# The down weights' block sums move from POOL's queue at the head into the gates' stage, and the fourth activation sum takes one transfer a block instead of two

## The chip, the cores and the metric

One core of one Trainium2 chip runs the whole kernel. The metric is the device time of one execution in microseconds (us), the median of the runs. The engines are TensorE (PE; its weight loads are listed as PEld), VectorE (DVE), ScalarE (ACT), GpSimd (POOL) and SyncE (SP). SP and POOL issue the DMA transfers; POOL issues all those that add to their destination.

## What is computed

One layer of a streaming encoder on 1024 prompt tokens and 64 sample tokens (1088 columns), model width 1024. Cut to what matters:

```python
mk, mv = split(rms_norm(mem, g_mem) @ w_mem_kv)                 # 256 memory tokens
h = rms_norm(x, g_mix_pre)
q, k, v, ca, cb, qm, ga, gb, gc = split(h @ w_in)               # nine widths of 1024
y_sb = stick_breaking(q, k, v) @ w_sb_o
u = ca * sigmoid(cb)                                            # conformer branch
cc = silu(layer_norm(causal_dwconv31(u) + conv_dw_b)); y_conv = cc @ w_conv_o
y_mem = memory_attention(qm, mk, mv) @ w_mem_o
merged = sigmoid(ga) * y_sb + sigmoid(gb) * y_conv + sigmoid(gc) * y_mem
x = x + rms_norm(merged @ w_out, g_mix_post)
up = rms_norm(x, g_ffn_pre) @ w_ffn_up                          # 2 x 2816 channels
fg, fv = split(causal_dwconv3(up))
y = x + rms_norm((gelu(fg) * fv) @ w_ffn_down, g_ffn_post)
```

The last product, (1088 x 2816) times (2816 x 1024), is done in the kernel as a two-by-two block product with seven block multiplications in place of eight. It needs sums of the four blocks of w_ffn_down (A and B are the upper and lower rows of columns 0 to 511, C and E those of columns 512 to 1023) and sums of the blocks of the activations.

## The kernel before, in words

All matrix products run in three passes of rounded halves: a weight block is loaded as `wraw` (SP, line 133), ScalarE casts the high half `whi` (`split`, line 103) and VectorE subtracts to get the low half `wlo` (line 104). `wraw` has three buffers, `whi` and `wlo` two each. `mms` (lines 160 to 162) issues the three matmuls of a step.

The stages, in the order of the program:

- **The head.** The keys and values of the memory tokens (`mem_kv`, matmuls at lines 374 to 376) take 16 blocks of w_mem_kv. Beside the first nine of them one tile of x each is loaded (`x_tile`, line 270), squared on ScalarE (line 276), given its reciprocal root on POOL in two small operations (`rstd_of`, lines 201 and 202, output `rstd_x`; `rstd_mem` for the memory tokens), scaled on VectorE (line 281), and turned on TensorE in groups of four tiles (`turn`, line 291, output `xT`), from which ScalarE and VectorE make the halves `hh` and `hl` of h (lines 107 and 108).
- **The gates' stage.** For each of eight channel blocks i the units cb, ca, qm, ga, gb, and then the eight gc: 48 dense products of h with columns of w_in. After ca of block i, `start_conv` lets POOL write the two edges of the convolution's input `u` (a memset at line 585 and a copy at line 586), and the 31 taps follow bit by bit: the first on ScalarE (line 424), 30 on VectorE (line 427, two at each chunk's end). `u` and its accumulator `acc` have two buffers each. The gc units carry the layer norm's pieces.
- **The attention stage.** `weave.mix` runs the projections of q, k and v and weaves scores, turns and values of the stick-breaking attention in between.
- The branches' output projections, the merge, w_out and the norms.
- **The channel stage.** For 22 blocks f of 128 channels, seven products each (lines 1490 to 1492), the convolution of width 3 (`conv`: POOL copies its edges at lines 1527 to 1529, VectorE taps at line 1532), gelu times value (line 1581), and `put_down`, which writes the block and its sums to DRAM tensors x11, x21, x22, t1 to t4 and small ones for the sample columns (`put` by SP, line 1546; `add`, an accumulating transfer by POOL, line 1549). Blocks 0 to 10 belong to the upper half and put; blocks 11 to 21 add.
- **The down stage**: seven block products (lines 1735 to 1737) that load the sums of weights (`d_w`, shown as d_ws by the profile) and of activations (`d_x`, its t1 to t4 shown as d_xt).

The sums of the weights' blocks are 32 transfers on POOL's queue: for each of s3 = A + C, s1 = C + E, s2 = A + s1 and s4 = B + s2 four plain copies of 352 rows by 512 columns from DRAM to DRAM (line 1123) and then four accumulating ones of the same size onto them (line 1125). An accumulating one must wait for the copy of its rows, and those of s2 and s4 also for the sum they take in. In the program text they are taken from a list one at a time inside `weave.mix`, in the attention stage:

```python
if i % 15 == 7 and down_sums:
    down_sums.pop(0)()
```

The order of instructions on an engine is not that of the text, though. A scheduler sets it by its own costs and by what each instruction depends on, but for places in the text under `tc.manual_schedule`, which keeps the named engine in the text's order. The transfers of the weights' sums depend on inputs alone, and in before the scheduler has put all 32 at the head of POOL's queue, among the rstd operations.

Of the kernel before, what the change touches and what calls it, by code (L numbers as in the profile page):

```python
# [12 lines left out]
ALU = mybir.AluOpType  # L13
# [41 lines left out]
def encoder_step(ctx: ExitStack, tc: tile.TileContext, I, O):  # L55
    nc = tc.nc
    ACT, DVE, POOL, PE, SP = nc.scalar, nc.vector, nc.gpsimd, nc.tensor, nc.sync
# [39 lines left out]
    HK = FF // 2  # L97
    d_w = {j: dp.tile([HK, 512], F32, name=f"d_w{j}") for j in ("s1", "s2", "s3", "s4")}
# [161 lines left out]
    with ExitStack() as st:  # L260
# [152 lines left out]
        def drain(n):  # L413
            owed[0] += n
            while owed[0] >= 1 and bg:
                bg.pop(0)()
                owed[0] -= 1
            owed[0] = min(owed[0], 1.0)

        def conv_ops(i, u):  # L420
            acc = ep.tile([P, 1118], F32, tag="acc", name=f"acc{i}", bufs=2)

            def first():
                ACT.activation(acc, u[:, 0:1118], AF.Identity, bias=cb_c[:, i : i + 1], scale=cw[:, i : i + 1])

            def tap(t):
                DVE.scalar_tensor_tensor(  # L427
                    out=acc, in0=u[:, t : t + 1118], scalar=cw[:, t * 8 + i : t * 8 + i + 1], in1=acc,
                    op0=ALU.mult, op1=ALU.add,
                )  # L430

            def last():
                SP.dma_start(out=d_cc[i * P : (i + 1) * P, 0:TP], in_=acc[:, 0:TP])
                SP.dma_start(out=d_cc[i * P : (i + 1) * P, TP:T], in_=acc[:, 1054:1118])

            return [first] + [lambda t=t: tap(t) for t in range(1, 31)] + [last]

        def conv_state(i, u):
            tp = bank("tr", f"cs{i}")
            PE.transpose(tp[:30, 0:P], u[:, 1024:1054], ident)  # L440
            PE.transpose(tp[:30, P : 2 * P], u[:, 1118:1148], ident)
            cs = ep.tile([30, 2 * P], F32, tag="cs", name=f"cso{i}", bufs=2)
            ACT.copy(out=cs, in_=tp[:30, : 2 * P])
            SP.dma_start(out=O["conv_state_prompt"][0, 0][:, i * P : (i + 1) * P], in_=cs[:, 0:P])
            SP.dma_start(out=O["conv_state_sample"][0, 0][:, i * P : (i + 1) * P], in_=cs[:, P : 2 * P])
# [92 lines left out]
        def step_mem(n=1):  # L538
            for _ in range(n):
                while mem_gens:  # L540
                    try:
                        next(mem_gens[0])
                        break
                    except StopIteration:
                        mem_gens.pop(0)
# [14 lines left out]
        def conv_b(i):  # L560
            sg = ep.tile([P, T], F32, tag="sg", name=f"sg{i}", bufs=1)
            u = ep.tile([P, 1148], F32, tag="u", name=f"u{i}", bufs=2)
            us[i] = (sg, u)

            def evac(ps, t0, n):
                ACT.activation(sg[:, t0 : t0 + n], ps, AF.Sigmoid)

            yield from dense(hT, CH, evac, f"cb{i}")

        def conv_a(i):  # L570
            sg, u = us[i]

            def evac(ps, t0, n):
                for o, m, c in segs(t0, n, 60):
                    c0 = c + 30 if c < TP else c
                    DVE.tensor_tensor(
                        out=u[:, c0 : c0 + m], in0=ps[:, o : o + m], in1=sg[:, t0 + o : t0 + o + m], op=ALU.mult
                    )

            yield from dense(hT, CH, evac, f"ca{i}")  # L580

        def start_conv(i):
            drain(len(bg))
            _, u = us.pop(i)
            POOL.memset(u[:, 0:30], 0.0)
            POOL.tensor_copy(out=u[:, 1054:1084], in_=cst[:, i * 30 : (i + 1) * 30])
            bg.extend(conv_ops(i, u))
            conv_state(i, u)
# [10 lines left out]
        def pace(g, ops):  # L599
            for _ in g:  # L600
                drain(ops)
                step_mem()
# [28 lines left out]
        def ep_tile(kind, shape, name, t):  # L631
# [4 lines left out]
            }[kind][t]  # L636
            return ep.tile(shape, F32, tag=tag, name=name, bufs=bufs)

        live = []
        ticks = 0  # L640
        order = ctx.enter_context(ExitStack())
        for nm, i in units:
            if nm == "cb":
                pace(conv_b(i), 2.2)
            elif nm == "ca":
                pace(conv_a(i), 2.2)
                start_conv(i)
            elif nm == "qm":
                pace(mem_q(i), 2.2)
                if i % 2:  # L650
                    mem_gens.append(mem_attention(i // 2, [qmh[i - 1], qmh[i]], [qml[i - 1], qml[i]]))
            elif nm == "gc":
                if i == 2:
                    order.enter_context(tc.manual_schedule(engines={mybir.EngineType.PE}))
                for end in gate(2, i, dense_steps):
                    if end:
                        step_mem()
                    if bg:
                        if end:
                            drain(3)  # L660
                        continue
                    ticks += 1
                    if ticks % 3 == 0:
                        if len(live) < 4 and len(norms) > 2:
                            live.append((0, layer_norm(norms.pop(0), ep_tile)))
                        if live and live[0][0] <= ticks:
                            g = live.pop(0)[1]
                            if next(g, 0) is None:
                                live.append((ticks + 12, g))
            else:  # L670
                pace(gate(("ga", "gb").index(nm), i), 1.8)
# [6 lines left out]
    with ExitStack() as st:  # L678
# [296 lines left out]
        class Weave:  # L975
# [115 lines left out]
            def mix(self, steps):  # L1091
                for i, _ in enumerate(steps):
                    if i % (3 * NK) == 0:
                        self.work((1024, 1024))
                    if i % 15 == 7 and down_sums:
                        down_sums.pop(0)()
                    self.now += self.STEP
                    while self.left() and self.take():
                        pass
# [12 lines left out]
                self.until(lambda: not self.left())  # L1112

        weave = Weave()


        w_dn = I["w_ffn_down"][0]
        A, B = (w_dn[HK * i : HK * i + HK, 0:512] for i in range(2))
        C, E = (w_dn[HK * i : HK * i + HK, 512:1024] for i in range(2))
        down_sums = []  # L1120
        for j, first, then in (("s3", A, C), ("s1", C, E), ("s2", A, d_w["s1"]), ("s4", B, d_w["s2"])):
            rows = [slice(HK // 4 * i, HK // 4 * i + HK // 4) for i in range(4)]
            down_sums += [lambda j=j, r=r, a=first: POOL.dma_start(out=d_w[j][r, :], in_=a[r, :]) for r in rows]
            down_sums += [
                lambda j=j, r=r, a=then: POOL.dma_start(out=d_w[j][r, :], in_=a[r, :], accum_op=ALU.add, max_dma_last_dim=2048)
                for r in rows
            ]

        def attend(p, S):
            units = []  # L1130
# [83 lines left out]
    op = right.enter_context(tc.tile_pool(name="op", bufs=1, side="right", reuse_waits="tile"))  # L1214
# [203 lines left out]
    for oi, t in enumerate(y_tiles):  # L1418
# [23 lines left out]
        if t not in (0, 2, 5):  # L1442
            then = THEN.get(group[0][0])
# [95 lines left out]
    LEFT, RIGHT, NEW = slice(0, 512), slice(512, 1024), slice(TP + 2, NO)  # L1539

    def put_down(f, g, free):

        r = slice(f % (NF // 2) * P, f % (NF // 2) * P + P)

        def put(j, src):
            SP.dma_start(out=(d_x.get(j) or d_s[j])[r, :], in_=src)

        def add(j, src):
            POOL.dma_start(out=(d_x.get(j) or d_s[j])[r, :], in_=src, accum_op=ALU.add)

        if f < NF // 2:
            put("x11", g[:, LEFT])
            put("x1", g[:, NEW])
            DVE.tensor_tensor(out=free[:, LEFT], in0=g[:, LEFT], in1=g[:, RIGHT], op=ALU.add)
            put("t1", free[:, LEFT])
            ACT.activation(free[:, RIGHT], free[:, LEFT], AF.Copy, scale=-1.0)
            put("t2", free[:, RIGHT])
            put("t4", free[:, RIGHT])
            ACT.activation(g[:, RIGHT.start : NO], g[:, RIGHT.start : NO], AF.Copy, scale=-1.0)
            put("t3", g[:, RIGHT])  # L1560
            put("xd", g[:, NEW])
        else:
            put("x21", g[:, LEFT])
            put("x22", g[:, RIGHT])
            put("x2", g[:, NEW])
            add("t4", g[:, LEFT])
            add("t2", g[:, RIGHT])
            add("t3", g[:, RIGHT])
            add("xd", g[:, NEW])
            add("t4", g[:, RIGHT])  # L1570

    def after(f, j):

# [260 lines left out]
```

## Time and profile before

| what | value |
|---|---|
| median of 3 runs | 2570.61 us (2566.13 to 2572.54) |
| the profiled execution | 2567.92 us |
| its span, first to last instruction | 2566.2 us |
| TensorE busy | 2378.3 us, 93% of the span |
| VectorE busy | 1762.4 us, 69% |
| ScalarE busy | 1101.5 us, 43% |
| POOL busy | 181.7 us, 7% |
| mean DMA rate | 124 GB/s |

The numbers come from one execution, taken by the hardware profiler. Busy time is the time in which an engine executes; register, branch, semaphore and DMA-issuing instructions are not counted in the shares, though the rows of the DMA issues are shown in the order of time. Rows of the page's second part cut the span in 40 slices of 64.2 us and give the busy share in tenths. In rows of groups, "out<-in" names the tiles, without buffer numbers; "A <- B" in the waits means that A's engine sat idle until B ended, "issue" that the profile shows no releaser. Matmuls are pipelined, so their printed durations overlap; the distance between starts is what one costs.

### The profile page before, as it was taken

What the parts mean: (1) busy time and instruction counts of PE and PEld (TensorE: products, weight loads), DVE (VectorE), ACT (ScalarE), POOL (GpSimd) and SP (SyncE); (2) the same over time, 40 slices, a digit from 0 to 9 for tenths busy, and PEclk for the clock granted to TensorE, in tenths of its full rate; (3) what the DMA queues carried; (4) which work ended last, traced back from release to release, by engine and by line L of the source; (5) the groups of instructions that cost most, each with busy time, mean ns of one, the idle gap of its engine ahead of it and who ended that gap; (6) DMA issues with size and microseconds to landing.
All of it is one profiled execution on the core that took longest, in us unless ns stands there. A gap on an engine that the chain in (4) does not pass through costs nothing.

```text
span 2566.2 us, 38158 instructions
## 1 busy us (share of the span) xinstructions
PE 2378.3 (93%) x15035; PEld 2258.1 (88%) x15035; DVE 1762.4 (69%) x2177; ACT 1101.5 (43%) x2035; POOL 181.7 (7%) x350
## 2 busy tenths in 40 slices
PE   2229999999999999999999999999899999998998
PEld 1118999999998999999998999997799999997887
DVE  1115878778786578888888934543898888876555
ACT  2124242424234566666767621213644443334432
POOL 1220000000000000000000000001111112220002
PEclk7569999999999999999999999999999999999999
DMA  7774222222225553333336446522233336659654
GB/s 210 180 171 126 68 72 90 64 90 68 85 65 151 159 134 95 81 88 82 87 95 161 134 139 217 185 92 74 83 107 118 115 112 127 127 97 283 221 179 148
DMA packets 319716, 319.40 MB, mean 124 GB/s; under 512 B 73855, under 2 KB 249107, under 8 KB 319537
## 3 DMA queue, kind: packets, MB, share of 16 engines
q1 hardware_dynamic: 302657, 282.00, 36.0%
q0 software_dynamic: 16880, 34.97, 7.5%
q8 instruction: 118, 1.93, 0.3%
q14 instruction: 61, 0.50, 0.1%
HBM read 206.20 MB, written 112.14 MB: 124 GB/s over the span
## 4 chain that ended last, share of the span: by engine, by line
PE 45%; issue 3%; DVE 2%; ACT 1%; POOL 1%; DMA 1%; DVEq 0%; POOLq 0%; ACTq 0%
PE ff L1490 5%; PE ff L1491 5%; PE ff L1492 5%; PE dn L1735 3%; PE dn L1737 3%; PE dn L1736 3%; PE cv L162 1%; PE sb L162 1%; PE sb L161 1%; PE cv L161 1%; PE cv L160 1%; PE sb L160 1%; PE mo L160 1%; PE mo L161 1%; PE mo L162 1%
## 5 line engine op out<-in xcount | busy, mean ns | idle before, releaser
L427 DVE SCALAR_TENSOR_TENSOR acc<-u,cw,acc 128x1118 f32<-128x1118 f32 x240 | 331.6, 1382 | 5.6
L103 ACT CAST whi<-wraw 128x1024 fp32r<-128x1024 f32 x112 | 118.0, 1054 | 335.4 <-PE cv L161 74.3
L820 DVE TENSOR_TENSOR_SCAN r<-r 128x128 f32<-128x128 f32 (+7 forms) x128 | 173.3, 1355 | 58.6 <-ACT r L816 58.0
L160 PE MATMUL g<-hh,whi 128*128 128x362 f32 (+1 forms) x576 | 193.0, 335 | 0.0
L162 PE MATMUL g<-hh,wlo 128*128 128x362 f32 (+1 forms) x576 | 190.6, 331 | 0.0
L161 PE MATMUL g<-hl,whi 128*128 128x362 f32 (+1 forms) x576 | 190.5, 331 | 0.0
L104 DVE TENSOR_TENSOR wlo<-wraw,whi 128x1024 fp32r<-128x1024 f32 x112 | 136.5, 1219 | 42.3 <-ACT whi L103 39.8
L1502 DVE TENSOR_TENSOR mf<-mf,ff 128x548 f32<-128x548 f32 (+1 forms) x161 | 110.3, 697 | 48.4 <-PE ff L1492 48.3
L376 PE MATMUL mkv<-wlo,mh 128*128 128x512 f32 x64 | 28.9, 459 | 114.2 <-DVE wlo L104 114.2
L1532 DVE SCALAR_TENSOR_TENSOR mf<-mf,fw 128x1090 f32<-128x1090 f32 x88 | 118.9, 1351 | 17.5 <-ACT mf L1530 16.6
L1735 PE MATMUL dn<-wh,xh 128*128 128x512 f32 x308 | 121.0, 393 | 6.7 <-ACT xh L103 6.6
L1737 PE MATMUL dn<-wh,xl 128*128 128x512 f32 x308 | 120.7, 392 | 0.3 <-DVE xl L104 0.3
L1736 PE MATMUL dn<-wl,xh 128*128 128x512 f32 x308 | 120.7, 392 | 0.2 <-DVE wl L104 0.2
L376 PEld LDWEIGHTS mkv<-wlo,mh 128*128 128x128 f32 x64 | 14.4, 225 | 118.9 <-DVE wlo L104 115.5
L815 ACT ACTIVATE be<-z 128x128 f32<-128x128 f32 (+2 forms) x192 | 95.7, 499 | 41.0 <-PE z L844 24.6
L160 PEld LDWEIGHTS g<-hh,whi 128*128 128x128 f32 x576 | 109.8, 191 | 0.2
L161 PEld LDWEIGHTS g<-hl,whi 128*128 128x128 f32 x576 | 109.4, 190 | 0.1
L162 PEld LDWEIGHTS g<-hh,wlo 128*128 128x128 f32 x576 | 109.1, 189 | 0.0
L104 DVE TENSOR_TENSOR atl<-aT,ath 128x512 fp32r<-128x512 f32 (+1 forms) x160 | 99.5, 629 | 10.0 <-ACT ath L103 9.1
L103 ACT CAST ath<-aT 128x512 fp32r<-128x512 f32 (+1 forms) x160 | 87.1, 550 | 42.6 <-PE aT L871 26.8
L281 DVE TENSOR_SCALAR x<-x,rstd_x 128x1024 f32<-128x1024 f32 (+1 forms) x9 | 6.8, 752 | 143.6 <-POOL rstd_x L202 142.8
L104 DVE TENSOR_TENSOR xl<-dr,xh 128x1024 fp32r<-128x1024 f32 (+1 forms) x42 | 47.6, 1134 | 76.4 <-ACT xh L103 76.1
(549 smaller groups left out, 8070.8 us busy)
## 6 DMA issues: line engine op xcount, KB each, us to landing
wraw<-in_w_in SPq DMA_DIRECT2D x72, 512.0 KB, 4.0
d_ws<-in_w_ffn_down POOLq DMA_DIRECT2D x24, 704.0 KB, 6.9
d_gate<-gt SPq DMA_DIRECT2D x24, 544.0 KB, 3.0
vw<-in_w_ffn_up SPq DMA_DIRECT2D x22, 512.0 KB, 3.9
gw<-in_w_ffn_up SPq DMA_DIRECT2D x22, 512.0 KB, 3.8
d_xt<-mf SPq DMA_DIRECT2D x44, 256.0 KB, 2.4
d_xt<-mf POOLq DMA_DIRECT2D x44, 256.0 KB, 6.3
dr<-d_ws SPq DMA_DIRECT2D x20, 512.0 KB, 4.5
```

The source lines that it names most:

```text
L103: ACT.copy(out=hi, in_=src)
L104: DVE.tensor_tensor(out=lo, in0=src, in1=hi.bitcast(F32), op=ALU.subtract)
L160: PE.matmul(ps, wh[:, k, :], rh[k][c], start=first, stop=False)
L161: PE.matmul(ps, wh[:, k, :], rl[k][c], start=False, stop=False)
L162: PE.matmul(ps, wl[:, k, :], rh[k][c], start=False, stop=last)
L427: DVE.scalar_tensor_tensor(out=acc, in0=u[:, t : t + 1118], scalar=cw[:, t * 8 + i : t * 8 + i + 1], in1=acc, op0=ALU.mult, op1=ALU.add,)
L820: DVE.tensor_tensor_scan(out=rv, data0=rv, data1=rv, initial=1.0, op0=ALU.mult, op1=ALU.min)
L1490: PE.matmul(ps, w[:, k, :], xh[:, k, :], start=k == 0, stop=False)
L1491: PE.matmul(ps, w[:, k, :], xl[:, k, :], start=False, stop=False)
L1735: PE.matmul(y, xh[:, i, c], wh[:, i, :], start=k == 0, stop=False)
L1736: PE.matmul(y, xh[:, i, c], wl[:, i, :], start=False, stop=False)
L1737: PE.matmul(y, xl[:, i, c], wh[:, i, :], start=False, stop=k == NF // 2 - 1)
```

## The change

It has two parts.

First, the list of the 32 transfers is made before the gates' stage, and six of them are taken from it after `start_conv(i)` for each i from 2 to 7 (six, six, six, six, six and two). From the start of the stage's loop to the first gc unit POOL is under `tc.manual_schedule`, so that its instructions there keep the order of the text. The lines in `weave.mix` go.

Second, in `put_down` for blocks 11 to 21, VectorE adds the left and the right half into a free tile, and one transfer adds that sum to t4, where two transfers added the halves one after the other.

```diff
+        w_dn = I["w_ffn_down"][0]
+        A, B = (w_dn[HK * i : HK * i + HK, 0:512] for i in range(2))
+        C, E = (w_dn[HK * i : HK * i + HK, 512:1024] for i in range(2))
+        down_sums = []
...
         order = ctx.enter_context(ExitStack())
+        pool_order = ctx.enter_context(ExitStack())
+        pool_order.enter_context(tc.manual_schedule(engines={mybir.EngineType.Pool}))
         for nm, i in units:
...
             elif nm == "ca":
                 pace(conv_a(i), 2.2)
                 start_conv(i)
+                if i > 1:
+                    for _ in range(6):
+                        if down_sums:
+                            down_sums.pop(0)()
...
             elif nm == "gc":
+                if i == 0:
+                    pool_order.close()
...
                 for i, _ in enumerate(steps):
                     if i % (3 * NK) == 0:
                         self.work((1024, 1024))
-                    if i % 15 == 7 and down_sums:
-                        down_sums.pop(0)()
...
-            add("t4", g[:, LEFT])
             add("t2", g[:, RIGHT])
             add("t3", g[:, RIGHT])
+            DVE.tensor_tensor(out=free[:, LEFT], in0=g[:, LEFT], in1=g[:, RIGHT], op=ALU.add)
+            add("t4", free[:, LEFT])
             add("xd", g[:, NEW])
-            add("t4", g[:, RIGHT])
```

What this makes of the order shows on POOL at three places. The first is the head of POOL's queue, right behind the constants, in before; d_ws_105, 103, 104 and 106 are s3, s1, s2 and s4, and rstd_x_302 and 309 belong to the first two tiles of x:

```order
L1123 DMA d_ws_105<-in_w_ffn_down 352x512 x4
L1125 DMA d_ws_105<-in_w_ffn_down 352x512 x4
L1123 DMA d_ws_103<-in_w_ffn_down 352x512 x2
L201 TENSOR_SCALAR rstd_x_302<-ms_x_300 128x1
L1123 DMA d_ws_103<-in_w_ffn_down 352x512
L202 TENSOR_TENSOR rstd_x_302<-rstd_x_302,mhalf 128x1
L1123 DMA d_ws_103<-in_w_ffn_down 352x512
L1125 DMA d_ws_103<-in_w_ffn_down 352x512
L201 TENSOR_SCALAR rstd_x_309<-ms_x_307 128x1
L1125 DMA d_ws_103<-in_w_ffn_down 352x512
L202 TENSOR_TENSOR rstd_x_309<-rstd_x_309,mhalf 128x1
```

At the same place in the change the rstd operations stand alone:

```order
L201 TENSOR_SCALAR rstd_x_302<-ms_x_300 128x1
L202 TENSOR_TENSOR rstd_x_302<-rstd_x_302,mhalf 128x1
L201 TENSOR_SCALAR rstd_x_309<-ms_x_307 128x1
L202 TENSOR_TENSOR rstd_x_309<-rstd_x_309,mhalf 128x1
L201 TENSOR_SCALAR rstd_x_316<-ms_x_314 128x1
```

All 32 transfers are gone from ahead of, between and behind the eleven pairs of rstd operations there. The second place is POOL's queue in the gates' stage. In before only the edge copies of the eight channel blocks stand there, here those of the third to the sixth:

```order
L585 MEMSET u_1862 128x30
L586 COPY u_1862<-cst 128x30
L585 MEMSET u_2442 128x30
L586 COPY u_2442<-cst 128x30
L585 MEMSET u_3010 128x30
```

and in the change, with the same blocks' edges:

```order
L585 MEMSET u_1864 128x30
L586 COPY u_1864<-cst 128x30
L646 DMA d_ws_105<-in_w_ffn_down 352x512 x4
L648 DMA d_ws_105<-in_w_ffn_down 352x512 x2
L585 MEMSET u_2450 128x30
L586 COPY u_2450<-cst 128x30
L648 DMA d_ws_105<-in_w_ffn_down 352x512 x2
L646 DMA d_ws_103<-in_w_ffn_down 352x512 x4
L585 MEMSET u_3024 128x30
```

Each group of six stands between the edge copies of one channel block and those of the next. The third place is POOL's queue at one of the blocks 11 to 21 of the channel stage, in before (d_xt_113 is t4, 111 t2, 112 t3):

```order
L1549 DMA d_xt_113<-mf 128x512
L1549 DMA d_xt_111<-mf 128x512
L1549 DMA d_xt_112<-mf 128x512
L1549 DMA d_sxd<-mf 128x64
L1549 DMA d_xt_113<-mf 128x512
```

and in the change:

```order
L1555 DMA d_xt_111<-mf 128x512
L1555 DMA d_xt_112<-mf 128x512
L1555 DMA d_sxd<-mf 128x64
L1555 DMA d_xt_113<-mf 128x512
```

Four transfers stand where five stood, and t4's comes last.

More of the change, by code (lines that the diff above doesn't have):

```diff
@@ L637, in ep_tile @@
             return ep.tile(shape, F32, tag=tag, name=name, bufs=bufs)
+        w_dn = I["w_ffn_down"][0]
+        A, B = (w_dn[HK * i : HK * i + HK, 0:512] for i in range(2))
+        C, E = (w_dn[HK * i : HK * i + HK, 512:1024] for i in range(2))
+        down_sums = []
+        for j, first, then in (("s3", A, C), ("s1", C, E), ("s2", A, d_w["s1"]), ("s4", B, d_w["s2"])):
+            rows = [slice(HK // 4 * i, HK // 4 * i + HK // 4) for i in range(4)]
+            down_sums += [lambda j=j, r=r, a=first: POOL.dma_start(out=d_w[j][r, :], in_=a[r, :]) for r in rows]
+            down_sums += [
+                lambda j=j, r=r, a=then: POOL.dma_start(out=d_w[j][r, :], in_=a[r, :], accum_op=ALU.add, max_dma_last_dim=2048)
+                for r in rows
+            ]
         live = []
@@ L1114, in encoder_step @@
         weave = Weave()
[L1117 to L1127, printed above, removed]
         def attend(p, S):
```

## The prediction

> **What bounds the kernel now.** I read the page's slices first, then the windows, the waits of the first 222 us, and last the instructions in order of time on POOL, VectorE and TensorE. The page shows one stretch in which TensorE is not full:
>
> ```profile
> PE   2229999999999999999999999999899999998998
> ```
>
> A slice is 64 us. From the fourth slice on TensorE is at 90% or nearly so; in the first three it is at two tenths. The windows put numbers on the two sides of that border, and the order of time gives the border itself, the first matmul of the gates' stage at 221.51:
>
> ```profile
> 0.00:222.00 222.00, 76.78 (x314) 59.26 (x315) 48.04 (x67) 52.30 (x86) 40.89 (x71) 0.68 0.73 184
> 222.00:640.00 418.00, 418.00 (x2561) 412.84 (x2560) 329.58 (x339) 141.22 (x231) 1.96 (x12) 1.00 0.24 76
> ```
>
> The columns are length, busy time of PE, PEld, DVE, ACT and POOL, the granted clock, the DMA share and GB/s. TensorE is busy 76.78 of the first 222 us, so it idles 145.2 there; in the 418 us after that it idles not at all. The waits of that first stretch (us in total, times, longest) say what it idled for:
>
> ```profile
> DVE x L281 <- POOL rstd_x L202: 142.8, 8, 45.0
> PE mkv L376 <- DVE wlo L104: 114.2, 3, 41.5
> PE xT L291 <- DVE x L281: 14.0, 4, 10.2
> PE memT L291 <- DMA mem<-in_mem_prompt: 11.0, 4, 7.2
> PE mkv L374 <- ACT mst L382: 2.1, 1, 2.1
> ```
>
> TensorE waits for VectorE's low halves of the weights, and VectorE, 142.8 us of it, for POOL's rstd of the token tiles. POOL's own rows of that time show why a two-instruction rstd takes that long:
>
> ```profile
> 65.67 0.66 POOL L1123 DMA_DIRECT2D d_ws<-in_w_ffn_down  x1 [4.46 <-issue]
> 66.35 0.61 POOL L202 TENSOR_TENSOR rstd_x<-rstd_x,mhalf 128x1 f32<-128x1 f32 x1
> 164.00 1.01 POOL L1125 DMA_DIRECT2D d_ws<-d_ws  x1 [5.34 <-issue]
> 171.18 0.95 POOL L1125 DMA_DIRECT2D d_ws<-d_ws  x1 [6.17 <-issue]
> 177.61 0.99 POOL L1125 DMA_DIRECT2D d_ws<-d_ws  x1 [5.17 <-issue]
> 178.28 0.93 POOL L202 TENSOR_TENSOR rstd_x<-rstd_x,mhalf 128x1 f32<-128x1 f32 x1
> ```
>
> Between and ahead of the small operations stand the transfers of the down weights' blocks, and POOL can issue one only every 6 to 7 us (164.00, 171.18, 177.61). An rstd queued behind them comes that late, and the engines behind it follow at once. VectorE scales the token tile at 179.25 and makes the weights' low half right behind it, and TensorE resumes after 41.47 us:
>
> ```profile
> 179.25 0.75 DVE L281 TENSOR_SCALAR x<-x,rstd_x 128x1024 f32<-128x1024 f32 x1 [45.00 <-POOL rstd_x L202]
> 179.92 1.22 DVE L104 TENSOR_TENSOR wlo<-wraw,whi 128x1024 fp32r<-128x1024 f32 x1
> 181.19 0.79 PE L376 MATMUL mkv<-wlo,mh 128*128 128x512 f32 x1 [41.47 <-DVE wlo L104]
> 181.78 0.63 PE L374 MATMUL mkv<-whi,mh 128*128 128x512 f32 x1
> 182.21 0.63 PE L375 MATMUL mkv<-whi,ml 128*128 128x512 f32 x1
> ...
> 185.19 0.63 PE L376 MATMUL mkv<-wlo,mh 128*128 128x512 f32 x1
> ```
>
> So the head of the kernel is bound by POOL's queue, and everything behind it by TensorE. The 32 transfers hold that queue over the whole head:
>
> ```profile
> L1123 POOL DMA_DIRECT2D d_ws<-in_w_ffn_down x16: 584/626/1062, 2.2 to 158.1; - x16
> L1125 POOL DMA_DIRECT2D d_ws<-in_w_ffn_down x8: 937/976/1029, 26.0 to 97.2; - x8
> L1125 POOL DMA_DIRECT2D d_ws<-d_ws x8: 955/1004/1058, 119.7 to 184.8; - x8
> ```
>
> From 2.2 to 184.8 there are 31 intervals, 5.9 us each.
>
> **What the change removes from the head.** All 32 transfers leave POOL's queue ahead of the rstd; the rest of the head stays in nearly the same order on every engine. What that frees, step by step:
>
> The two waits that hang on POOL, 114.2 + 14.0 = 128.2 us, go. The 2.1 us for the bank of the memory keys is between TensorE and ScalarE and stays.
>
> The start: TensorE waits 11.0 us for the memory tokens while two of POOL's transfers (352 x 512 values, 704 KB each, together 1.44 MB) share the DMA engines. At the rate of that time they take 3.9 us of it:
>
> ```profile
> 10.00:20.00 10.00, 4.21 (x16) 3.48 (x17) 3.52 (x6) 4.07 (x7) 1.18 (x2) 1.00 1.00 365
> 194.00:222.00 28.00, 28.00 (x139) 21.56 (x138) 17.75 (x29) 14.94 (x29) 0.86 (x4) 0.95 0.55 164
> ```
>
> 1.44 MB at 365 GB/s is 3.9 us; I take 2, between 0 and 4.
>
> The clock: the restart at 181.19 runs its matmuls 0.43 us apart (181.78 to 182.21), and they stay so to 185.19, ten of them. Matmuls of the same shape, with no stall ahead, stand 0.234 apart (ten steps from 218.94 to 221.28):
>
> ```profile
> 138.98 0.50 PE L374 MATMUL mkv<-whi,mh 128*128 128x512 f32 x1 [2.14 <-ACT mst L382]
> ...
> 192.91 0.77 PE L374 MATMUL mkv<-whi,mh 128*128 128x512 f32 x1
> 218.94 0.40 PE L375 MATMUL mkv<-whi,ml 128*128 128x512 f32 x1
> 221.28 0.39 PE L376 MATMUL mkv<-wlo,mh 128*128 128x512 f32 x1
> 221.51 0.33 PE L160 MATMUL cb<-hh,whi 128*128 128x364 f32 x1
> ```
>
> Ten at 0.196 each is 2 us for a restart, and there are four long stalls (three of 114.2, one of 10.2), so at most 8 us. I take 4, since some restart will be left.
>
> What is late next: the loads of weights and tokens, and the chain load, cast, low half. The last seven of the 16 weight blocks took 28.6 us (192.91 to 221.51), 4.1 a block with all the transposes between them, and TensorE was busy 28.00 of 28 us there, so 164 GB/s of loads kept up with it. The first nine blocks come with a token tile each, about 1 MB for a block; at the 365 GB/s of the window from 10 to 20 us that is 2.9 us, less than 4.1. Still some waits will show which POOL's covered: three weight buffers, a token tile that lands late, an rstd between square and scale. I price them at 6 us, a pause of 3 for each of the two groups of four token tiles, and bound them at 0 and 30 (2 for every one of 15 blocks, the size of the wait at 138.98).
>
> The head's sum: 128.2 + 2 + 4 - 6 = 128.2 us less, so the gates' stage would start near 93.
>
> **What it adds to the gates' stage.** TensorE is full there, so only what makes it wait costs. POOL's queue gets six transfers behind the edge copies of each channel block from the third on; at 5.9 us a group takes 35 us. In before, the edge copies themselves stand like this, with the first reader of one of them on ScalarE:
>
> ```profile
> 294.62 0.12 POOL L585 MEMSET u<- 128x30 f32 x1 [77.78 <-DVE acc L427]
> 294.68 0.21 POOL L586 COPY u<-cst 128x30 f32<-128x30 f32 x1
> 631.18 0.12 POOL L585 MEMSET u<- 128x30 f32 x1 [65.13 <-DVE sm L482]
> 380.34 1.32 ACT L424 ACTIVATE acc<-u,vec,cw 128x1118 f32<-128x1118 f32 x1
> ```
>
> From 294.62 to 631.18 are five intervals of 67.3 us, and the copy done at 294.9 is first read at 380.34, 85 us later. A group of 35 us fits the interval, and behind that stand 85 us of slack, so POOL delays nobody. The wait that the change adds is each accumulating transfer's for the copy of its rows; queued behind it on POOL are only the next edge copies, and for them waits ScalarE's first tap. The DMA engines are at a share of 0.24 here. Weight loads may land later, but they have room:
>
> ```profile
> 308.03 0.38 SPq L133 DMA_DIRECT2D wraw<-in_w_in  x1
> 346.15 1.06 ACT L103 CAST whi<-wraw 128x1024 fp32r<-128x1024 f32 x1 [3.22 <-issue]
> DMA to landing us min/median/max: 3.8/3.9/6.2
> 2130.00:2180.00 50.00, 50.00 (x396) 50.00 (x395) 42.66 (x54) 18.05 (x25) 14.83 (x25) 1.00 0.63 134
> ```
>
> The load issued at 308.03 has the buffer that the cast of 305 to 308 freed and is cast as the third from there, at 346.15: 38 us for a landing of 3.9. And the channel stage shows TensorE 50.00 of 50 us busy at a DMA share of 0.63, with POOL's accumulating transfers in it. I price this part at 0 and leave its failure to a rival.
>
> The Trainium skill has a rule against this place: its page "SBUF — State Buffer", section "SBUF: two separate sides", says that GpSimd cannot write its descriptors while VectorE runs a copy in its two-port mode, and gives 620 ns grown to about 3100. An estimate from that page is 2.5 us more for each transfer, 15 for a group, and so still no change of the sum. The trace speaks against it: the small transfers of L1549 (867 to 898 ns, row below) take no longer with VectorE 42.66 of 50 us busy than the block transfers of the idle head (955 to 1058).
>
> **What it changes in the channel stage.** For each of the last eleven blocks POOL issues one accumulating transfer less, and VectorE adds one 128x512 sum, whose like takes 0.69 us:
>
> ```profile
> L1470 DVE TENSOR_TENSOR wsh<-vw x22: 684/692/694, 1823.2 to 2268.1; 128x512 f32<-128x512 f32 x22
> L1549 POOL DMA_DIRECT2D d_sxd<-mf x11: 866/876/898, 2118.0 to 2335.1; - x11
> ```
>
> That is 7.6 us on VectorE under a full TensorE (42.66 beside 50.00 above): nothing, and 7.6 if that cover were gone. The eleven transfers less free POOL of some 10 us that nobody waited for. 0, between -1 and +1.
>
> **The rivals.**
>
> *The clock stays low.* If each weight block of the new head starts after a pause long enough, TensorE runs the whole head at 0.43 a matmul. For it: every restart after a long stall is slow, the first matmul at 181.19 taking 0.79 and the one at 192.91 0.77. Against it: after 2.14 us of idling the one at 138.98 takes 0.50, and the last seven blocks ran at 0.234. The price: 192 matmuls at 0.196 more are 37.6 us, of which the head of before already pays 8, so 29.6, and my 4 go too: 128.2 - 33.6 = 94.6 us less. It decides from pauses between 2.14 and 10 us at every block. By the Trainium skill's page "TensorE: Matmul & The Clock Gate", section "Part 1: The HAM clock gate (the "warmup" mystery)", about 3.4 us without work halves the clock; the two idle times here lie on either side of that, so the trace agrees as far as it goes.
>
> *The groups of six don't fit.* If a transfer in the gates' stage takes much longer than in the head, the next edge copies come late behind it, ScalarE's first tap waits in front of all the evictions of its queue, and TensorE stops. Five groups have edge copies behind them. The delay is five times what a group is over 67.3 us, less the 85 of slack; it eats the whole gain at 67.3 + (85 + 128) / 5 = 110 us a group, 18.3 a transfer. At 25 us a transfer (150 a group) it would be 328 us, 200 more than the gain. For it: transfers and weight loads share the engines all through the stage. Against it: 5.9 us was the pace at a DMA share of 0.73, and no row is near 18.
>
> *Nothing is freed.* The head's length could hang on the loads, with POOL only the last in the list of waiters. Against it: the row at 179.25 names POOL as what ended the 45.00 us, and the low half and the matmul follow it at once. Then the time stays.
>
> That the change doesn't do what it says is no rival: the order shows the transfers behind the edge copies, and no other engine's rows moved but for a few in the head and eleven sums.
>
> **How the numbers follow.** The profiled execution took 2567.9 us (2566.2 of span, 1.7 around it); the median of the three runs is 2570.6, 2.7 above. 2567.9 - 128.2 + 2.7 = 2442.4 us. Forecast 0.80, the low clock 0.13 (2570.6 - 94.6 = 2476), the long groups 0.04 (2771), nothing freed 0.03 (2570.6). The forecast's own bounds: 128.2 + 4 + 8 + 1 - 0 = 141 us less, 2430, and 128.2 + 0 + 0 - 30 - 1 = 97 less, 2473. The low clock's end, 2476, is taken in, and its gain can be a little greater: the range is 2428 to 2477. A measurement of this kernel tells 0.3%, 8 us, from no change; so faster 0.93, the same 0.03, slower 0.04.
>
> **What would show it.** In the new profile TensorE's first matmul of the gates' stage (cb<-hh) should stand near 93 us, with the waits of VectorE for POOL's rstd down from 142.8 to a few us and those of TensorE for the low halves from 114.2 to under 30. The gates' stage should still be 418 us for the same rows, TensorE full, the DMA share above 0.24, and a group of six on POOL 35 to 45 us long. The channel stage should be as long as before. The forecast is wrong if long gaps remain in the first 93 us whose releaser is a load, if the granted clock there is near 0.5, or if ScalarE's first tap waits for POOL.

## The result, and the profile after

| what | before | after |
|---|---|---|
| median (lowest to highest), 4 runs each | 2571.06 us (2566.13 to 2572.54) | 2416.61 us (2413.64 to 2418.31) |
| profiled execution, its span | 2567.92, 2566.2 us | 2413.64, 2411.9 us |
| first matmul of the gates' stage | 221.51 us | 72.09 us |
| first matmul of the down stage's products | 2324.5 us | 2169.8 us |

The ratio is 0.9401 [0.9385, 0.9417], a gain of 154.5 us by the medians and of 154.3 by the spans. The forecast was 2442.4 us, a gain of 128.2, and its range ended at 2428: the direction and the mechanism came as forecast, the time lies 11 us below the range. All but 5 us of the gain is already there when the gates' stage begins: 221.51 - 72.09 = 149.4.

Of the page after the change, the two rows of slices that answer to the row of before with its 222 at the start:

```profile
PE   8999999999999999999999999999999999999998
PEclk9999999999999999999999999999999999999999
```

TensorE is at 90% or more from the second slice to the last but one (a slice is 60.3 us), at full clock. The windows put numbers on the head and on the 418 us behind it (length, busy time of PE, PEld, DVE, ACT and POOL, granted clock, DMA share, GB/s). For the head of before I take the window up to its own border:

```profile
0.00:221.50 221.50, 76.28 (x311) 58.77 (x312) 47.60 (x66) 51.80 (x85) 40.89 (x71) 0.68 0.73 184
```

and of after the head and the gates' stage:

```profile
0.00:72.00 72.00, 64.08 (x311) 50.68 (x312) 47.09 (x66) 49.88 (x85) 13.32 (x39) 1.00 0.74 246
72.00:490.00 418.00, 418.00 (x2559) 412.79 (x2558) 329.60 (x339) 141.71 (x232) 26.14 (x43) 1.00 0.50 130
```

The same 311 matmuls of the head take TensorE 64.1 us instead of 76.3, and its idle time falls from 145.2 to 7.9. The gates' stage is as full as before, though the DMA share there has gone from 0.24 to 0.50. The waits of the head are now short (us in total, times, longest), of VectorE for POOL 5.2 in place of 142.8:

```profile
DVE x L281 <- POOL rstd_x L202: 5.2, 7, 0.9
PE memT L291 <- DMA mem<-in_mem_prompt: 4.7, 3, 2.5
PE vecT L303 <- DMA grow<-in_g_mem: 2.5, 1, 2.5
PE xT L291 <- DVE x L281: 0.6, 1, 0.6
```

TensorE's whole list in the head is the last three rows. Its waits for the low halves (114.2) and for the memory keys' evictions (2.1) don't stand in it any more. In order of time, POOL now starts the second half of an rstd 0.3 us behind the first, and ScalarE's square is what it waits for:

```profile
18.41 0.22 POOL L201 TENSOR_SCALAR rstd_x<-ms_x 128x1 f32<-128x1 f32 x1 [2.94 <-ACT junk_x L276]
18.71 0.57 POOL L202 TENSOR_TENSOR rstd_x<-rstd_x,mhalf 128x1 f32<-128x1 f32 x1
```

And the first group of six stands where the change put it, behind the third block's edge copies:

```profile
145.25 0.21 POOL L586 COPY u<-cst 128x30 f32<-128x30 f32 x1
145.79 1.48 POOL L646 DMA_DIRECT2D d_ws<-in_w_ffn_down  x2 [0.34 <-issue]
153.45 0.60 POOL L646 DMA_DIRECT2D d_ws<-in_w_ffn_down  x1 [6.17 <-issue]
155.48 0.58 POOL L646 DMA_DIRECT2D d_ws<-in_w_ffn_down  x1 [1.43 <-issue]
161.36 1.03 POOL L648 DMA_DIRECT2D d_ws<-in_w_ffn_down  x1 [5.30 <-issue]
169.83 0.95 POOL L648 DMA_DIRECT2D d_ws<-in_w_ffn_down  x1 [7.44 <-issue]
210.04 0.12 POOL L585 MEMSET u<- 128x30 f32 x1 [39.26 <-DVE sm L482]
```

The six are issued within 25 us, and the four groups of six behind them within 26 to 35, where the prediction looked for 35 to 45. POOL then stands idle 39 us until the next edge copies may begin. Those wait for VectorE, not for a transfer.

### The profile page after: what moved, and what is told of

It is laid out like the page before. It is cut to its first block, busy times and chain, and to the rows that moved or that the text cites. A ratio compares the mean times of both kernels' runs of the same rounds, so it can differ in the third digit from the quotient of the medians.

```text
span 2411.9 us, 38148 instructions
## 1 busy us (share of the span) xinstructions
PE 2362.2 (98%) x15035; PEld 2246.0 (93%) x15035; DVE 1767.9 (73%) x2188; ACT 1099.4 (46%) x2035; POOL 174.7 (7%) x339
## 4 chain that ended last, share of the span: by engine, by line
PE 49%; issue 2%; DVE 2%; ACT 1%; POOL 1%; DMA 1%; DVEq 0%; POOLq 0%; ACTq 0%; SPq 0%
PE ff L1496 6%; PE ff L1497 6%; PE ff L1498 6%; PE dn L1741 3%; PE dn L1743 3%; PE dn L1742 3%; PE sb L162 1%; PE cv L162 1%; PE cv L161 1%; PE sb L161 1%; PE cv L160 1%; PE sb L160 1%; PE mo L160 1%; PE mo L161 1%; PE mo L162 1%
## 5 line engine op out<-in xcount | busy, mean ns | idle before, releaser
L842 DVE TENSOR_TENSOR be<-be,r 128x127 f32<-128x127 f32 (+7 forms) x128 | 96.1, 753 | 2.7
L837 ACT ACTIVATE r<-z 128x128 f32<-128x128 f32 (+2 forms) x192 | 96.0, 500 | 0.0
L103 ACT CAST xh<-dr 128x1024 fp32r<-128x1024 f32 (+1 forms) x42 | 41.2, 982 | 99.7 <-PE dn L1742 96.6
```

The source lines that it names most:

```text
L103: ACT.copy(out=hi, in_=src)
```

## The experiments

The theory: POOL's queue is served in order, so 32 transfers at its head hold back the small rstd behind them; moved behind the edge copies, they have slack there. Its rivals: the gain comes from the second part of the change (t4); it comes from DMA engines that the head no longer shares; or the gates' stage pays for the transfers, and the head gave more than is seen. Times are compared with runs of before on the same chip, with medians of 2567.2 us (the first three kernels below and the one with all 32 in one group) and 2567.45 us (the other three).

**The move alone.** Of the change only t4's two transfers are put back:

```diff
+            add("t4", g[:, LEFT])
             add("t2", g[:, RIGHT])
             add("t3", g[:, RIGHT])
-            DVE.tensor_tensor(out=free[:, LEFT], in0=g[:, LEFT], in1=g[:, RIGHT], op=ALU.add)
-            add("t4", free[:, LEFT])
             add("xd", g[:, NEW])
+            add("t4", g[:, RIGHT])
```

> Only the move of the 32 transfers; t4 keeps its two transfers a block. If POOL's queue at the head is the cause, nearly the whole gain is here: 2417 us, at most 3 above the changed kernel. If the channel stage's part brought the 3 to 5 us by which the stages behind the head came out shorter, 2420 to 2422.

Measured 2417.66 us (2413.91 to 2418.07), ratio 0.9421 [0.9406, 0.9435]; the gates' stage begins at 72.4. That is 149.5 us less than before on its chip, against 154.5 for the whole change; the intervals of the two ratios overlap (0.9406 to 0.9435 here, 0.9385 to 0.9417 there), and the two kernels' medians lie 1.1 us apart. The move has all of the gain that can be told from the spread.

**The sum alone.** The same lines of t4 changed in the kernel before, and nothing else:

```diff
-            add("t4", g[:, LEFT])
             add("t2", g[:, RIGHT])
             add("t3", g[:, RIGHT])
+            DVE.tensor_tensor(out=free[:, LEFT], in0=g[:, LEFT], in1=g[:, RIGHT], op=ALU.add)
+            add("t4", free[:, LEFT])
             add("xd", g[:, NEW])
-            add("t4", g[:, RIGHT])
```

> Only the one t4 transfer a block; the 32 transfers stay at the head of POOL's queue. If it hides under TensorE, 2571 us, within 2 of before. If it had a share in the gain, 2566 to 2568.

Measured 2564.48 us (2562.74 to 2570.31, 10 runs), ratio 0.9995 [0.9984, 1.0007]. The interval reaches from 4 us less to 2 us more, so the second part is worth nothing that can be measured, as it was priced.

**The transfers stay at the head, the rstd leave POOL.** This parts the order of the queue from the shared DMA engines. In the kernel before, VectorE makes the head's eleven rstd by Newton steps and the edges of the first two blocks, so that nothing which the head needs stands in POOL's queue:

```diff
-            return rstd_of(ms, n, ep, f"rstd_{name}", tag, bufs)
+            r = ep.tile([P, 1], F32, tag=tag, name=f"rstd_{name}", bufs=bufs)
+            q = ep.tile([P, 1], F32, tag="ms", name=f"nr_{name}", bufs=4)
+            DVE.tensor_scalar(out=r[:n], in0=ms[:n], scalar1=-0.5, scalar2=1.5, op0=ALU.mult, op1=ALU.add)
+            for _ in range(2):
+                DVE.scalar_tensor_tensor(out=q[:n], in0=r[:n], scalar=ms[:n, 0:1], in1=r[:n], op0=ALU.mult, op1=ALU.mult)
+                DVE.tensor_scalar(out=q[:n], in0=q[:n], scalar1=-0.5, scalar2=1.5, op0=ALU.mult, op1=ALU.add)
+                DVE.tensor_tensor(out=r[:n], in0=r[:n], in1=q[:n], op=ALU.mult)
+            return r
...
+            edge = DVE if i < 2 else POOL
```

> The 32 transfers stay at the head of POOL's queue, but nothing of the head waits for that queue any more: the eleven rstd are made on VectorE by two Newton steps (eps left out), and the edge copies of the first two channel blocks on VectorE too. If the order of POOL's queue was the cause, the head shrinks though the transfers are in it: first matmul of the gates' stage at 75 to 90 us, time 2420 to 2440; what is above the changed kernel is then the price of the shared DMA engines and some 12 us of small VectorE operations. If the transfers lengthened the head by taking the DMA engines from the loads, the gates' stage starts after 150 us and the time stays above 2490.

Measured 2433.27 us (2429.71 to 2438.77), ratio 0.9487 [0.9466, 0.9507]. The gates' stage begins at 90.7, just behind the 75 to 90 that were expected. So 221.5 - 90.7 = 130.8 us of the head's 149.4 hang on the order of POOL's queue. The transfers still start at 2.2 us; 13 of the 32 are issued inside the shorter head, the others after it. The remaining 18.6 us belong to those 13, and to the small operations put on VectorE, which this kernel doesn't part. Its waits in the first 120 us:

```profile
ACT whi L103 <- DMA wraw<-in_w_mem_kv: 16.8, 5, 4.8
PE memT L298 <- DMA mem<-in_mem_prompt: 11.0, 4, 7.0
PE mkv L381 <- ACT mst L389: 3.7, 1, 3.7
PE mkv L381 <- ACT whi L103: 3.5, 2, 3.0
```

The wait for the memory tokens is 11.0 us again, as in before, and 4.7 in after: in these traces 6.3 us are the transfers' share of the DMA engines at the start. And now weight blocks come late (16.8), in a head with a DMA share of 0.96:

```profile
0.00:80.00 80.00, 55.64 (x257) 43.33 (x258) 49.03 (x129) 44.10 (x68) 9.38 (x24) 0.98 0.96 292
```

**A long queue on POOL without a transfer.** The reverse: the change as it is, with 40 memsets of an unused tile ahead of each of the eleven rstd, and POOL kept in the text's order in the head:

```diff
+    head_order = ExitStack()
+    head_order.enter_context(tc.manual_schedule(engines={mybir.EngineType.Pool}))
...
+            for _ in range(40):
+                POOL.memset(fw, 0.0)
             return rstd_of(ms, n, ep, f"rstd_{name}", tag, bufs)
...
+        head_order.close()
         pool_order = ctx.enter_context(ExitStack())
```

> The changed kernel with 40 small memsets on POOL ahead of each of the eleven rstd of the head and no transfer there: the queue is late, the DMA engines are free. At 0.15 us each a filler takes 6 us, so the rstd come about 6.8 us apart and the one of the last full token tile at 2 + 10 x 6.8 = 70 us, against 42.4 in the changed kernel. If a late queue alone makes the long head, the gates' stage starts some 27 us later, near 99, with VectorE waiting for POOL's rstd again: 2435 to 2455 us, and the granted clock below 1.00 in the head if its pauses are long enough. If it takes the transfers' load on the DMA engines, 2417.

Measured 2487.91 us (2486.46 to 2492.26), ratio 0.9694 [0.968, 0.9709], above what was expected: 40 memsets take 11.08 us, where 6 had been priced, and the gates' stage begins at 134.4, where 99 had been expected. An rstd comes every 12.0 us, here those of the second and the third in the queue:

```profile
14.34 11.08 POOL L281 MEMSET fw<- 128x132 f32 x40
25.51 0.22 POOL L204 TENSOR_SCALAR rstd_x<-ms_x 128x1 f32<-128x1 f32 x1
25.82 0.57 POOL L205 TENSOR_TENSOR rstd_x<-rstd_x,mhalf 128x1 f32<-128x1 f32 x1
26.34 11.08 POOL L281 MEMSET fw<- 128x132 f32 x40
37.51 0.22 POOL L204 TENSOR_SCALAR rstd_x<-ms_x 128x1 f32<-128x1 f32 x1
```

and with them the waits of the first 148 us and the low clock of before are back:

```profile
DVE x L286 <- POOL rstd_x L205: 38.0, 9, 11.2
PE xT L296 <- DVE x L286: 36.0, 7, 10.9
```

```profile
0.00:148.00 148.00, 90.71 (x337) 69.62 (x338) 53.38 (x70) 56.21 (x89) 105.95 (x479) 0.72 0.41 134
```

The DMA share is 0.41 here, in before's head 0.73, so a late POOL alone makes a long head and a low clock.

**All 32 in one group.** The slack behind the edge copies, overdrawn:

```diff
-                if i > 1:
-                    for _ in range(6):
+                if i == 1:
+                    for _ in range(32):
```

> The changed kernel with all 32 transfers behind the edge copies of the second channel block, in place of groups of six. At 6.3 us a transfer POOL is held from 67 to about 268 us; the third block's edge copy is due at its first tap near 231. By the law of the rival on long groups ScalarE's first tap then stops some 37 us with the evictions behind it, and TensorE after it: 2440 to 2453 us, with a gap of TensorE in the gates' stage that names ScalarE. If POOL's queue is off the path there whatever its length, 2417.

Measured 2437.57 us (2435.36 to 2443.54), ratio 0.9505 [0.9487, 0.9523], 21 us above after and just under the 2440 to 2453 that were expected. The transfers run from 66.49 to 250.30, 31 intervals of 5.9 us where 6.3 had been priced, so POOL is free 17 us sooner than expected. The third block's edge copies stand behind them:

```profile
250.30 0.93 POOL L648 DMA_DIRECT2D d_ws<-d_ws  x1 [6.05 <-issue]
250.88 0.48 POOL L585 MEMSET u<- 128x30 f32 x1
```

ScalarE's first tap then waits for the edges, and in its queue behind the tap stands a softmax piece of the memory attention, for which VectorE and then TensorE wait:

```profile
251.53 1.32 ACT L424 ACTIVATE acc<-u,vec,cw 128x1118 f32<-128x1118 f32 x1 [21.39 <-POOL u L586]
254.41 0.47 ACT L478 ACTIVATE mp0s<-msc0s,mx0s 64x256 f32<-64x256 f32 x1
```

```profile
257.51 0.44 PE L520 MATMUL mpT0s<-ident,mp0s 64*128 64x64 f32 x2 [19.37 <-DVE mp0s L484]
```

The memset that stands at 145.2 in after is 105.7 us late. Less the 85 us of slack that the prediction read from before, that is 20.7, and TensorE stopped for 19.4. The rule of the prediction's second rival is right; it is the size of a group that keeps the change clear of it.

**No transfers.** The down stage loads unsummed blocks in place of s1 to s4, so the sums are left out:

```diff
-                if i > 1:
-                    for _ in range(6):
-                        if down_sums:
-                            down_sums.pop(0)()
...
-        (A, "x11", "x1"), (B, "x21", "x2"), (d_w["s2"], "t2", None), (d_w["s3"], "t3", None),
-        (d_w["s1"], "t1", "x1"), (E, "t4", "xd"), (d_w["s4"], "x22", None),
+        (A, "x11", "x1"), (B, "x21", "x2"), (A, "t2", None), (C, "t3", None),
+        (C, "t1", "x1"), (E, "t4", "xd"), (B, "x22", None),
```

> The changed kernel without the 32 transfers at all; the down stage loads unsummed blocks of the weights in the sums' place, so the output isn't the reference's. If the transfers cost nothing in the gates' stage, 2416 us, the same as the changed kernel within 3. If they still slow it there, by later weight loads, faster by more than that: 2400 to 2411.

Measured 2416.47 us (2414.75 to 2418.53), ratio 0.9414 [0.9398, 0.943]. Without the work nothing is won: the 32 transfers cost nothing that can be measured in their new place.

**Every transfer twice.** Groups of twelve, each of the four sums made twice:

```diff
+        down_sums = [f for b in range(0, 32, 8) for f in down_sums[b : b + 8] * 2]
...
-                    for _ in range(6):
+                    for _ in range(12):
```

> The changed kernel with every transfer made twice (copy, add, copy, add), in groups of twelve. At 6 us a transfer a group takes 72 to 76 us, up to 9 over the interval of 67.3; five groups add up to 45 at most, less than the 85 of slack, so by the law of the long groups no wait: 2416 us, within 3. If the engines' share already matters, twice the transfers show it: 2425 or more. If the slack is smaller than I read it, a TensorE gap late in the gates' stage that names ScalarE or VectorE.

Measured 2415.4 us (2414.32 to 2415.48), ratio 0.9408 [0.9394, 0.9422]. The window of the gates' stage, of the kernel without transfers and of the one with twice as many:

```profile
72.00:490.00 418.00, 418.00 (x2561) 412.83 (x2560) 329.59 (x339) 141.09 (x232) 1.95 (x12) 1.00 0.24 77
```

```profile
72.00:490.00 418.00, 418.00 (x2561) 412.83 (x2561) 329.32 (x338) 141.10 (x233) 49.49 (x72) 1.00 0.72 177
```

TensorE is busy 418.00 of 418 us at DMA shares of 0.24, 0.50 and 0.72. With twice the transfers the edge copies do come late (the seventh block's memset at 432.24, in after at 416.4), and a weight block lands 7.9 us after its issue in the median, in after 4.4. Both stay inside their slack.

## Why the prediction was wrong

The spans differ by 154.3 us, of which 149.4 lie ahead of the gates' stage. By the prediction's own terms for the head, with its price and what the two traces show:

| term | priced (bounds) | measured |
|---|---|---|
| waits on POOL, 114.2 + 14.0 | 128.2 | 127.6 |
| start | 2 (0 to 4) | 6.3 |
| clock | 4 (0 to 8) | 12.1 |
| what is late next | -6 (-30 to 0) | 0; its 0.6 us is in the first row |
| the 2.1 us of the memory keys | 0 | 2.1 |
| other waits at the start | 0 | 1.4 |
| sum | 128.2 | 149.5 |

Of the 21.3 us that the sum was short, 8.1 are the clock, 6.0 the price for what is late next, 4.3 the start, and 3.5 waits that it put at nothing; the waits on POOL give 0.6 back.

- **The waits on POOL** went as forecast: 114.2 to nothing, 14.0 to 0.6. The kernels with the rstd on VectorE and with the filled queue show from both sides that it was the queue's order.
- **The start, mis-sized.** I divided the bytes of two transfers by the rate of the window, 3.9 us, and halved that. TensorE's first matmul of the memory keys moved from 17.64 to 11.66, and the wait for the memory tokens fell by 6.3; with the transfers at the head and the rstd on VectorE it is 11.0 again. But it is not the same in every execution. The kernel with t4 alone has the transfers in the same place and waits less:

```profile
PE memT L291 <- DMA mem<-in_mem_prompt: 7.7, 4, 4.1
```

  The six kernels without them at the head wait 3.9 to 5.3. So the term lies between 2.4 and 7.1 us, and in two of three traces the bytes over the rate were no upper bound for what a transfer ahead does to a load behind it. How the packets of the two share the engines I have not measured.
- **The clock, mis-sized.** "Ten at 0.196 each is 2 us for a restart, and there are four long stalls." The trace of before has a fifth slow restart, and its row stood in the prediction, at 192.91, taken for one after a long stall: it comes behind three pauses of TensorE, each under 1.6 us, with transposes between them (granted clock 0.89 from 185.6 to 190, 0.50 from there to 196.5). The groups of the head show what that left out, in before:

```profile
L374 PE MATMUL mkv<-whi,mh 128*128 128x512 f32 x64 | 30.7, 480 | 2.1 <-ACT mst L382 2.1
L375 PE MATMUL mkv<-whi,ml 128*128 128x512 f32 x64 | 29.4, 459 | 0.0
L376 PE MATMUL mkv<-wlo,mh 128*128 128x512 f32 x64 | 28.9, 459 | 114.2 <-DVE wlo L104 114.2
L291 PE MATMUL xT<-ident,x 128*128 128x128 f32 (+1 forms) x72 | 13.3, 325 | 14.0 <-DVE x L281 14.0
```

  and in after (busy, mean ns of one, then the idle time before them):

```profile
L374 PE MATMUL mkv<-whi,mh 128*128 128x512 f32 x64 | 27.1, 423 | 0.0
L375 PE MATMUL mkv<-whi,ml 128*128 128x512 f32 x64 | 26.4, 413 | 0.0
L376 PE MATMUL mkv<-wlo,mh 128*128 128x512 f32 x64 | 25.4, 406 | 0.0
L291 PE MATMUL xT<-ident,x 128*128 128x128 f32 (+1 forms) x72 | 9.6, 272 | 0.6 <-DVE x L281 0.6
```

  The 192 matmuls of the memory keys and values lose 10.1 us (89.0 to 78.9) by these durations, which overlap, and 9.1 by the distances between starts, more than the bound of 8; the 72 transposes of x, which I didn't count at all, another 3.7, or 2.9 by the distances. TensorE's busy time fell by 12.1. My 4 also kept half of the restarts, and none is left: only the start of after still runs slow, from 11.66 to 15.22. (The clock records of a trace begin with the first rise, so the 1.00 of the window doesn't hold it.)
- **What is late next, mis-sized.** I expected a 3 us pause at each group of token tiles and bounded the sum at 30. It was 0.6. In after no wait of TensorE behind the memory tokens names a load, at a DMA share of 0.74 for the head. The bandwidth sum of the prediction (2.9 us for a block's loads against 4.1 of matmuls) had already said so, and I priced against it.
- **The 2.1 us of the memory keys, wrong.** I had read one link: TensorE waits for ScalarE. ScalarE's own row in before names the next one:

```profile
138.24 0.69 ACT L382 ACTIVATE mst<-mkv,rstd_mem 128x512 f32<-128x512 f32 x1 [3.34 <-POOL rstd_mem L202]
```

  It waited for POOL's rstd of the memory tokens, so it went with the others.
- **The gates' stage at nothing, right.** Three transfer loads (none, 32, 64) give 2416.5, 2416.6 and 2415.4 us. The Trainium skill's rule against this place ("SBUF — State Buffer", section "SBUF: two separate sides", a transfer issued by GpSimd that takes 620 ns alone and some 3100 beside a VectorE copy) shows in no run here: an accumulating issue takes 0.93 to 1.03 us in after, with VectorE busy 329.6 of 418 us, as in the head of before, and the transfers from w_ffn_down land 7.2 us after their issue in the median, in before 6.9. But VectorE makes no copy there (248.6 of the 329.6 us are the taps), so the rule isn't put to the test. (The 867 ns that the prediction gives for L1549 are 866 in its row.)
- **The channel stage and t4 at nothing, right.** The kernel with t4 alone is within its interval of no change.
- **The rivals.** The low clock didn't come: in after's head no pause of TensorE behind the start is longer than 0.58 us. The filled queue shows that its condition was rightly named, since there TensorE runs at half speed after each pause of 2.76 us and more. That nothing is freed is refuted by the head of 72.09 us. Groups that don't fit are shown by the kernel with one group.

What stays open are the last 4.9 us, which lie behind the head: after's 2339.8 us from the start of the gates' stage to the end against before's 2344.7. The move alone has 2343.2 there, the kernel without transfers 2342.9 and t4 alone 2342.1. So no edit is seen to carry them, and single executions differ by as much. They come in steps of 1.6 us or less: 1.5 up to the first q product, 1.6 in the channel stage, 1.2 in the wait ahead of the down stage. A part may be the clock: behind the head, up to the last matmuls, before's trace has it at one half for 20.5 us and after's for 10.2, which is worth at most 5.1 us. The move alone has 23.9 us of it and t4 alone 20.5, so the times don't follow it strictly, and this stays a guess.

## What to carry to other kernels

A transfer on a compute engine's queue costs that queue a slot as long as the pace of the transfers (5.9 us in the mean here), so a small operation that others wait for should not stand behind a row of them; look for a later stage in which the queue's next customer has slack, and work out group length against interval plus slack before moving them. When such a wait is removed, everything that it made slow comes back too: count every slow restart and every kind of matmul, follow each remaining wait down to its last link, and don't take a term for "something will be late next" against a bandwidth sum that says it won't.

## What was not expected of the hardware

- A restart's slow phase has no fixed length, though the clock changes in fixed steps. Matmuls of the same shape stand 0.43 us apart from 11.66 to 15.22 in after, 3.6 us. In the kernel with the filled queue it is 5.4 us after a pause of TensorE of only 2.76 us that had four transposes behind it:

```profile
83.03 0.39 PE L380 MATMUL mkv<-whi,ml 128*128 128x512 f32 x1
86.18 1.09 PE L296 MATMUL xT<-ident,x 128*128 128x128 f32 x4 [2.76 <-DVE x L286]
86.92 0.78 PE L381 MATMUL mkv<-wlo,mh 128*128 128x512 f32 x1
87.49 0.63 PE L379 MATMUL mkv<-whi,mh 128*128 128x512 f32 x1
...
91.76 0.62 PE L380 MATMUL mkv<-whi,ml 128*128 128x512 f32 x1
92.18 0.42 PE L381 MATMUL mkv<-wlo,mh 128*128 128x512 f32 x1
92.44 0.40 PE L379 MATMUL mkv<-whi,mh 128*128 128x512 f32 x1
```

  Each trace keeps records of the granted clock, and these change only in whole steps of 3.413 us. In before's head the clock is at one half for 40.96, 34.13, 13.65, 44.37 and 6.83 us in turn, and full for 3.41, 3.41, 13.65 and 3.41 between them. In all five restarts it rises at the second such step behind TensorE's first instruction, 3.9 to 6.0 us later (181.19 to 186.30, for one). It can also fall in a step that is not idle: in the rows above it is at one half from 85.4 on, and in the step before that (82.0 to 85.4) TensorE is busy for 1.4 us.

  The Trainium skill's page "TensorE: Matmul & The Clock Gate", section "Part 1: The HAM clock gate (the "warmup" mystery)", gives some 3.4 us of time for the slow phase, whatever the number of matmuls, in a window that runs on by itself. The steps of the trace agree with such a window, and so does the phase of 3.6 us; the one of 5.4 is longer. The prediction took from the same section of the Trainium skill that about 3.4 us without work halve the clock; the pause of 2.76 us in which it falls here is shorter.
- The accumulating transfers on POOL come further apart where the DMA engines are full. In the full head of the kernel with the rstd on VectorE (DMA share 0.96) they stand 15.0 and 12.5 us apart, in the gates' stage of after (DMA share 0.50) 6.9 to 9.1:

```profile
25.36 1.02 POOL L1133 DMA_DIRECT2D d_ws<-in_w_ffn_down  x1 [8.42 <-issue]
40.36 0.94 POOL L1133 DMA_DIRECT2D d_ws<-in_w_ffn_down  x1 [13.98 <-issue]
52.87 0.94 POOL L1133 DMA_DIRECT2D d_ws<-in_w_ffn_down  x1 [11.57 <-issue]
```
